# A two-layer hybrid decoder trunk: seven changes to the order of work around the norm, the first attention, the last retention and the end

## The chip, the core and the metric

The kernel runs on one core of a Trainium2 chip. A core has several engines that run side by side, each with its own queue of instructions: TensorE (PE) multiplies matrices into PSUM banks and loads its stationary operand separately (PEld), VectorE (DVE) and ScalarE (ACT) do elementwise work, GpSimd (POOL) does the same more slowly, and SyncE (SP) issues the transfers between memory and the core's on-chip buffers. The metric is the device time of one execution in microseconds (us); lower is better.

## What is computed

The reference, cut to what matters. There are 528 tokens (16 meta tokens and 512 of the sequence), a width of 1024, two layers, 8 attention heads of 64 and 4 retention heads of 128.

```python
def hybrid_layer(h, attn_norm_g, w_in, b_fgate, ret_gn_g, w_out,
                 ffn_norm_g, w_gate, w_up, w_down, cos, sin):
    xn = rmsnorm(h, attn_norm_g)
    proj = jnp.einsum('bld,dc->blc', xn, w_in)
    fq, fk, fv, flog, rq, rk, rv, rg = jnp.split(proj, SPLIT_POINTS, axis=-1)
    logf = jax.nn.log_sigmoid(flog.astype(jnp.float32) + b_fgate.astype(jnp.float32))
    fox_out = fox_attention(fq.reshape(fshape), fk.reshape(fshape), fv.reshape(fshape), logf)
    rq_ = rotate(rq.reshape(rshape), cos, sin)
    rk_ = rotate(rk.reshape(rshape), cos, sin) * (RET_HEAD_DIM ** -0.5)
    ret = retention_chunkwise(rq_, rk_, rv.reshape(rshape))
    ret = head_groupnorm(ret, ret_gn_g).astype(h.dtype)
    ret_out = jax.nn.silu(rg) * ret
    mix = jnp.concatenate([fox_out, ret_out], axis=-1)
    h = h + jnp.einsum('blc,cd->bld', mix, w_out)
    hn = rmsnorm(h, ffn_norm_g)
    ff = jax.nn.silu(jnp.einsum('bld,df->blf', hn, w_gate)) * jnp.einsum('bld,df->blf', hn, w_up)
    return h + jnp.einsum('blf,fd->bld', ff, w_down)
```

The attention adds the cumulative sum of `logf` to its scores: `logit[t,s] = q_t.k_s/sqrt(Dh) + c[t] - c[s]`. After the two layers a last rmsnorm is applied and the meta tokens are dropped.

## The kernel before

Activations lie with their features on the 128 partitions and the tokens along the row: `h` is 8 tiles of 128x528. For precision every operand of a matmul is split into a rounded high part and a rest (`split`, L142: a cast on ACT, a subtraction on DVE), and a product is three matmuls: high by high, rest by high, high by rest. Weights are split in the same way (`whi` by ACT, `wlo` by POOL or DVE; L192, L195) from a ring of three fetched blocks `raw` (L159).

A **dense step** (L218) is the product of one 128-row chunk of a weight block with one chunk of the activations: three matmuls for each of the two halves of the 528 tokens. Eight steps make a block of 128 outputs. Each layer runs four groups of columns, then the output projection, then the feed-forward part.

The order of PE is the order of the program text (`tc.manual_schedule`, L1350): the list `plan` in `layer` (L1247) holds all steps of a layer, and `run` (L233) issues them one by one. The order of the other engines is made by a scheduler, which follows the program but moves forward what stands under `tc.high_priority()`, and leaves alone what `pin` (L308) keeps in program order. So where PE's steps stand also sets where the work behind them stands on ACT and DVE.

The parts of a layer that matter here:

- **Start and norm.** `squares` (L327) sums the squares of `h`; `first_parts` (L1310) splits the sum into `sqh` and `sql`; `rstd` adds it over the partitions with two matmuls (L291) and makes the norm factor `R` by a logarithm (L296), an exponential (L297) and one Newton step on DVE (L298 to L301). Dense steps don't wait for `R`; it is applied to their results. `qk` is the list of the query and key steps of the first pair of attention heads, a query and a key step in turn, 16 in all; `v` holds the 8 value steps.
- **Gates.** `forget_gates` (L369, matmuls L381) multiplies out the 8 forget gates; two copies (L387) and two additions (L388) join the two halves of each result into `z`. `forget_sums` (L391) scales `z` by `R`, takes the log sigmoid, and scans it along the tokens (L401). The sums go to memory (`cdr`), and each head's row comes back as a broadcast over 128 partitions, `bc` (L501).
- **Attention** (`fox_steps`, L474), for a pair of heads: `values` transposes the values in five matmuls (L420) and splits them into `vv` (L487, L488); `scores` (L511) for a block of queries, with a mask (L517), a reduction with `bc` on DVE (L518) and an exponential on ACT (L531); block -1 is that of the meta tokens, with four small operations of its own (L547, L548, L557, L559); `turn` transposes and splits the weights into `pth` and `ptl`; `product` (L584) multiplies them with the values.
- **Retention** (`ret_steps`, L666): `values` (L420 again, then L680 and L681), `scores` (L717), `product` (L751, and L748 as its last matmul), a head norm with the same `col_rstd` (statistics L291, then L296, L297, L298 to L301, L787), `weigh` (L780, times the gate, whose `silu` is L409), and `gate`, which splits the result into a mix tile `mxh`, `mxl`. The mix tiles are what the output projection multiplies.
- **Places.** `merge` (L247) puts these steps among the dense steps: a step with the place 7 goes ahead of the eighth dense step of its stretch. `spread(main, a, b)` spreads a list evenly over the places from a to b. `ret_places` gives ten places: values, the first two scores, first product, third scores, two products, and last weigh, head norm and gate.
- **PSUM.** Results lie in two rings: `psd`, two pairs of banks for dense steps, and `psa`, four banks for everything else. A step that takes a bank waits until the last reader of the step four allocations earlier is done.
- **End.** The last norm is worked out in two parts of columns. For the second part (240 columns), `square_b` squares each tile (L1130), `sum_b` adds five of them up in `acc` (L1133), and three stay single. `sums` (L1159) adds over the partitions, `root` (L1147) and `newton` (L1151, L1153, L1155) make the factor, `out` multiplies (L1137) and sends (L1138). `after_0` to `after_7` stand behind the units of the last product, whose results are added to `h` by L1095.

ACT holds one table of functions at a time. Logarithm, exponential and `silu` are not all in one table; where the next function needs another, an `ACT_TABLE_LOAD` stands ahead of it.

Of the kernel before, what the change touches and what calls it, by code (L numbers as in the profile page):

```python
# [10 lines left out]
F32 = mybir.dt.float32  # L11
F32R = mybir.dt.float32r
AF = mybir.ActivationFunctionType
ALU = mybir.AluOpType
# [25 lines left out]
def hybrid_kernel(ctx, tc, x_t, w_in, w_fl, w_out, w_gate, w_up, w_down, vecs, b_fg, rope, decay, mask, ident, out_t):  # L40
    nc = tc.nc
# [15 lines left out]
    bfg = const.tile([FH, DEPTH], F32, name="bfg")  # L57
# [202 lines left out]
    def psum_a():  # L260
        return psa.tile([128, 512], F32, name="psa", tag="psa")
# [65 lines left out]
    def squares(st, cols, pinned=False, att=True):  # L327
        c = slice(cols[0][0], cols[-1][1])
        acc = tt("ss")
        for k in range(NK):  # L330
            if k == 0:
                first = nc.scalar.activation(acc[:, c], h[0][:, c], AF.Square)
                if pinned:
                    tc.keep_in_program_order(first)
            else:
                sq = tt("sq")
                more = nc.scalar.activation(sq[:, c], h[k][:, c], AF.Square)
                if pinned:
                    tc.keep_in_program_order(more)
                with ExitStack() if att else tc.high_priority():  # L340
                    nc.vector.tensor_add(acc[:, c], acc[:, c], sq[:, c])
        if pinned:
            st["acc"] = acc
            return
        with ExitStack() if att else tc.high_priority():
            st["parts"] = col_parts(acc, cols)
# [44 lines left out]
    def forget_sums(l, st):  # L391
        z = st["z"]
        z2 = tt("z2")[0:FH]
        with ExitStack() if l else tc.high_priority():
            nc.vector.scalar_tensor_tensor(z, z, RSC, st["R"][0:FH, :], ALU.mult, ALU.mult)
            nc.scalar.activation(z2, z, AF.Abs, bias=bfg[:, l:l + 1])
            nc.scalar.activation(z2, z2, AF.Exp, scale=-1.0)
            nc.scalar.activation(z2, z2, AF.Ln, bias=onec[0:FH])
        nc.vector.tensor_scalar(z, z, bfg[:, l:l + 1], 0.0, ALU.add, ALU.min)
        nc.vector.tensor_sub(z, z2, z)  # L400
        nc.vector.tensor_tensor_scan(z2, z, z, 0.0, ALU.add, ALU.max)  # L401
        st["cdr"] = tc.dram_tile([FH, T], F32, name=f"cdr{l}")
        nc.sync.dma_start(st["cdr"], z2)

# [410 lines left out]
    def ffn(l, st, real, last):  # L815
# [269 lines left out]
        else:  # L1085
# [4 lines left out]
            na, nb = PA[1] - PA[0], PB[1] - PB[0]  # L1090
            fin = {}
# [40 lines left out]
            def sum_b(m):  # L1132
                pin(nc.vector.tensor_add(fin["acc"], fin["acc"], fin["sq", m]))  # L1133
# [6 lines left out]
            def out_a(k):  # L1140
                out(fin["ya"][k // HB][:, k % HB:k % HB + 2], fin["ra"], k, *PA)
# [15 lines left out]
            def sums(v, parts):  # L1157
                for i, t in enumerate(parts):
                    nc.tensor.matmul(v, ones if t.dtype == F32R else ones.bitcast(F32), t, start=(i == 0), stop=(i == len(parts) - 1))  # L1159
# [39 lines left out]
            def after_4():  # L1199
                sum_b(3)  # L1200
                square_b(4)
                out_a(2)
                scale_b(1)

            def after_5():
                sum_b(4)
                square_b(5)
                hi, lo = tt("sqh", F32R)[:, 0:nb], tt("sql", F32R)[:, 0:nb]
                pin(nc.scalar.copy(hi, fin["acc"]))
                fin["b"] = hi, lo  # L1210
                scale_b(2)

            def after_6():
                hi, lo = fin["b"]
                pin(nc.vector.tensor_sub(lo, fin["acc"], hi.bitcast(F32)))
                square_b(6)

            def after_7():
                hi, lo = fin["b"]
                square_b(7)  # L1220
                v = psum_a()[:, 0:nb]
                sums(v, (fin["one"][0], hi, lo, fin["one"][1], fin["one"][2]))
                out_a(4)
                out_a(6)
                scale_b(3)
                root(fin["rb"], v)
                scale_b(4, 5, 6, 7)
# [19 lines left out]
    def layer(l):  # L1247
# [3 lines left out]
        ly, ff = {"wait": []}, {}  # L1251
# [19 lines left out]
        plan = []  # L1271
# [42 lines left out]
        sums = [lambda: forget_sums(l, ly)]  # L1314
        plan = [lambda: enter_att(l), start]
        if l == 0:
            plan += [lambda: squares(ly, FULL, True, False)] + qk[:6] + qk[6:] + [first_parts] + gates + stats + [lambda: ly["wait"].pop(0)()] + sums + [lambda: ly["wait"].pop(0)()]
        else:
            plan += [lambda: squares(ly, FULL)] + q[:7] + stats + q[7:] + gates + sums + k
        plan += v + [ropes]  # L1320

        def ret_places(hd, *places):

            f = rs[hd]
            return list(zip(places, (f[0], f[1], f[2], f[4], f[3], f[5], f[6], f[7], f[8], f[9])))

        for g in range(2):
            main, rest = fs[g]
            m0, r0, places = (((7, 31), (34, 40.5), (13, 33.5, 35.5, 37.5, 39, 40.5, 43, 44, 47.5, 48)),
                              ((0.5, 31.5), (32, 40), (13, 33.5, 35.5, 39.5, 39, 41.5, 43, 44, 47.5, 48)))[g]  # L1330
            plan += merge(rd(g, "vqkg") + sum(fd(g + 1), []),
                          spread(main, *m0), spread(rest, *r0), ret_places(g, *places))
# [7 lines left out]
        base += op[0:3] + op[4:7] + op[8:11] + op[12:15]  # L1340
        plan += merge(base, spread(main, 2, 46.5), spread(rest, 51, 56),
                      ret_places(2, 26, 23.5, 24.5, 32, 28, 33.5, 36, 56.5, 40.5, 57.5),
                      ret_places(3, 52, 45.5, 47.5, 57.5, 55.5, 58.5, 60, 64.1, 63, 64.2))
        plan += [op[3], op[7], op[11], op[15]] + op[16:]
        up = ffn(l, ff, real, real)
        plan += [lambda: enter("ffn"), start_ffn] + up
# [2 lines left out]
    plan = [f for l in range(DEPTH) for f in layer(l)]  # L1349
# [75 lines left out]
```

## Time and profile before

| | |
|---|---|
| time, median of 3 runs | 1272.59 us (1272.03 to 1273.82) |
| the profiled execution | span 1270.1 us |
| instructions | 23589 |
| PE busy | 1252.6 us |
| DVE busy | 1003.8 us |
| ACT busy | 694.5 us |
| POOL busy | 263.3 us |
| longest waits of PE | 1.7 us (product, L584), 1.6 us (first matmul of the program, L1278), 1.6 us (values, L420) |

The span of the profiled execution begins with its first instruction and ends with its last, and the times of the table's first row contain what lies around it. In the rows of the timeline that the prediction shows, the first number is the start in us from the start of the span, the second the duration of the group, then come the engine, the line of the program, the operation, the output and the inputs by their names in the program, the shapes, and the number of instructions in the group; in brackets stands how long the engine idled ahead of it and what ended that. Groups overlap slightly, since instructions are pipelined.

### The profile page before, as it was taken

The page shows a single profiled execution, that of the slowest core. Times are in us where ns is not written, and L with a number is a line of the kernel's source. Part 1 is how long each engine was busy: PE and PEld are TensorE (multiplying, and loading weights), DVE is VectorE, ACT ScalarE, POOL GpSimd, SP SyncE. Part 2 cuts the span into 40 slices and gives each one's busy share as a digit, 9 for nine tenths or more (in the row PEclk, how much of TensorE's full clock was granted, in tenths as well). Part 3 has the DMA queues.
Part 4 walks back from the last instruction along what each step waited for, and adds up shares of the span by engine and source line. Part 5 has one row for each costly group of instructions (what it writes and reads, how often), then busy time and mean ns, then how long its engine had stood idle before and what let it go on. Part 6 is the DMA issues. An engine that isn't in the chain of part 4 may idle for free.

```text
span 1270.1 us, 23589 instructions
## 1 busy us (share of the span) xinstructions
PE 1252.6 (99%) x9225; PEld 1193.1 (94%) x9225; DVE 1003.8 (79%) x1866; ACT 694.5 (55%) x1284; POOL 263.3 (21%) x524
## 2 busy tenths in 40 slices
PE   9999999999999999999999999999999999999997
PEld 8899999999999999999998989998789999999996
DVE  7877856879988888887786877568899888888867
ACT  7666556676444444444465665457764444444445
POOL 3355546420000000000025546454100000000000
PEclk9999999999999999999999999999999999999999
DMA  6322222213323232322323122221223333333321
GB/s 218 93 68 84 83 94 75 68 68 116 106 96 100 100 100 100 100 100 84 101 76 114 63 101 84 77 91 67 100 91 126 101 100 101 100 100 100 100 84 67
DMA packets 45679, 120.56 MB, mean 95 GB/s; under 512 B 5360, under 2 KB 12272, under 8 KB 45568
## 3 DMA queue, kind: packets, MB, share of 16 engines
q1 hardware_dynamic: 45136, 118.77, 28.3%
q8 instruction: 72, 1.18, 0.4%
q14 instruction: 39, 0.32, 0.1%
q10 hardware_dynamic: 432, 0.29, 0.1%
HBM read 116.91 MB, written 2.13 MB: 94 GB/s over the span
## 4 chain that ended last, share of the span: by engine, by line
PE 89%; DVE 5%; ACT 4%; DMA 1%; issue 1%; ACTq 0%; DVEq 0%; SPq 0%
PE psd L218 27%; PE psa L902 18%; PE psd L1037 14%; PE psd L902 13%; PE psa L218 5%; PE psa L1037 4%; PE psa L420 2%; PE psa L511 1%; PE psa L584 1%; PE psa L717 1%; PE psa L751 1%; DMA bc<-cdr 1%; PE psa L381 1%; ACT whi L192 1%; DVE pr L518 0%
## 5 line engine op out<-in xcount | busy, mean ns | idle before, releaser
L195 POOL TENSOR_TENSOR wlo<-raw,whi 128x128 fp32r<-128x128 f32 x504 | 259.1, 550 | 288.8 <-ACT whi L192 287.3
L218 PE MATMUL psd<-xh,whi 128*128 128x264 f32 (+1 forms) x792 | 195.6, 314 | 0.4 <-ACT whi L192 0.4
L218 PE MATMUL psd<-xl,whi 128*128 128x264 f32 (+1 forms) x792 | 186.3, 302 | 0.6 <-DVE xl L321 0.6
L218 PE MATMUL psd<-xh,wlo 128*128 128x264 f32 (+1 forms) x792 | 186.7, 303 | 0.0
L218 PEld LDWEIGHTS psd<-xh,whi 128*128 128x128 f32 x792 | 128.2, 189 | 5.2 <-ACT whi L192 0.8
L218 PEld LDWEIGHTS psd<-xh,wlo 128*128 128x128 f32 x792 | 127.0, 188 | 6.3 <-DVE wlo L195 0.6
L218 PEld LDWEIGHTS psd<-xl,whi 128*128 128x128 f32 x792 | 127.6, 189 | 5.2 <-DVE xl L321 1.2
L192 ACT CAST whi<-raw 128x512 fp32r<-128x512 f32 (+1 forms) x168 | 98.2, 613 | 45.7 <-PE psd L218 31.5
L890 ACT CAST whi<-raw 128x1024 fp32r<-128x1024 f32 (+2 forms) x62 | 54.8, 884 | 50.3 <-PE psd L902 37.0
L890 ACT CAST fwhi<-raw 128x1024 fp32r<-128x1024 f32 (+2 forms) x62 | 55.6, 897 | 47.9 <-PE psd L902 40.1
L891 DVE TENSOR_TENSOR fwlo<-raw,fwhi 128x1024 fp32r<-128x1024 f32 (+2 forms) x62 | 64.0, 1032 | 11.7 <-ACT fwhi L890 11.6
L85 POOL MEMSET kl<- 64x528 f32 x2 | 1.1, 534 | 345.5 <-PE psa L902 345.5
L891 DVE TENSOR_TENSOR wlo<-raw,whi 128x1024 fp32r<-128x1024 f32 (+2 forms) x62 | 62.9, 1014 | 12.2 <-ACT whi L890 12.1
L902 PE MATMUL psa<-th,whi 128*128 128x264 f32 (+1 forms) x232 | 65.4, 282 | 0.0
L902 PE MATMUL psa<-th,wlo 128*128 128x264 f32 (+1 forms) x232 | 65.4, 282 | 0.0
L902 PE MATMUL psa<-tl,whi 128*128 128x264 f32 (+1 forms) x232 | 65.3, 282 | 0.0
L902 PE MATMUL psa<-th,fwhi 128*128 128x264 f32 (+1 forms) x224 | 63.4, 283 | 0.0
L902 PE MATMUL psa<-tl,fwhi 128*128 128x264 f32 (+1 forms) x224 | 63.3, 283 | 0.0
L902 PE MATMUL psa<-th,fwlo 128*128 128x264 f32 (+1 forms) x224 | 63.2, 282 | 0.0
L531 ACT ACTIVATE pr<-pr,nmax 128x144 f32<-128x144 f32 (+1 forms) x64 | 36.9, 576 | 43.2 <-DVE nmax L518 31.2
L890 ACT CAST fwhi<-S 128x1024 fp32r<-128x1024 f32 x20 | 21.0, 1049 | 68.6 <-PE psa L902 66.5
L968 ACT COPY e<-psa 128x264 f32<-128x264 f32 (+1 forms) x114 | 42.9, 376 | 27.7 <-PE psa L902 23.6
(356 smaller groups left out, 4036.6 us busy)
## 6 DMA issues: line engine op xcount, KB each, us to landing
raw<-w_in SPq DMA_DIRECT2D x54, 512.0 KB, 3.5
raw<-w_gate SPq DMA_DIRECT2D x44, 512.0 KB, 4.0
fraw<-w_up SPq DMA_DIRECT2D x38, 512.0 KB, 3.4
raw<-w_down SPq DMA_DIRECT2D x64, 256.0 KB, 2.7
raw<-w_out SPq DMA_DIRECT2D x16, 512.0 KB, 3.4
raw<-w_down SPq DMA_DIRECT2D x32, 192.0 KB, 2.5
bc<-cdr SPq DMA_DIRECT2D x16, 264.0 KB, 3.4
raw<-w_up SPq DMA_DIRECT2D x6, 512.0 KB, 3.5
```

Source lines behind the costliest of these rows:

```text
L192: pin(nc.scalar.copy(hi, job["raw"][:, c0:c1]), pinned)
L195: pin(sub(lo[:, c:c + step], job["raw"][:, c0 + c:c0 + c + step], hi[:, c:c + step].bitcast(F32)), pinned)
L218: nc.tensor.matmul(ps[1][b][:, 0:c1 - c0], w[:, wk, :], x[:, c0:c1], start=(k == 0 and i == 0), stop=(k == n - 1 and i == 2))
L381: nc.tensor.matmul(ps[:, 0:c1 - c0], wf[k // HB][:, k % HB, :], st["x"][k][part][:, c0:c1], start=(i == 0), stop=(i == 2 * NK - 1))
L420: nc.tensor.transpose(ps[:, 128 * j:128 * j + 128], src[:, o:o + 128], idt)
L511: nc.tensor.matmul(sc[0:nq, 0:c1 - c0], st["q"][s][:, q0:q0 + nq], kk[:, c0:c1], start=(i == 0), stop=(i == 1))
L531: nc.scalar.activation(pr, pr, AF.Exp, bias=nmax[0:nq], scale=-1.0, accum_out=rsum)
L890: nc.scalar.copy(hi, src)
L891: nc.vector.tensor_sub(lo, src, hi.bitcast(F32))
L902: nc.tensor.matmul(bank()[:, 0:b.shape[-1]], a[:, o + k, :], b, start=(fresh and k == 0 and i == 0), stop=(k == n - 1 and i == 2), skip_gr ...
L968: nc.scalar.copy(self.t["e"][:, i], self.t["x"][:, 0:w])
L1037: nc.tensor.matmul(v[:, 0:c1 - c0], a[:, s * n + k, :], b[:, c0:c1], start=(k == 0 and i == 0), stop=(k == n - 1 and i == 2))
```

## The change

Seven places of the order, and the operand of one sum.

```diff
     def forget_sums(l, st):
-        with ExitStack() if l else tc.high_priority():
+        with tc.high_priority():
             nc.vector.scalar_tensor_tensor(z, z, RSC, st["R"][0:FH, :], ALU.mult, ALU.mult)
...
-        nc.vector.tensor_scalar(z, z, bfg[:, l:l + 1], 0.0, ALU.add, ALU.min)
-        nc.vector.tensor_sub(z, z2, z)
-        nc.vector.tensor_tensor_scan(z2, z, z, 0.0, ALU.add, ALU.max)
+            nc.vector.tensor_scalar(z, z, bfg[:, l:l + 1], 0.0, ALU.add, ALU.min)
+            nc.vector.tensor_sub(z, z2, z)
+            nc.vector.tensor_tensor_scan(z2, z, z, 0.0, ALU.add, ALU.max)
...
             def after_4():
                 sum_b(3)
                 square_b(4)
-                out_a(2)
                 scale_b(1)
             def after_5():
+                square_b(5)
+                scale_b(2)
+
+            def after_6():
                 sum_b(4)
-                square_b(5)
-                hi, lo = tt("sqh", F32R)[:, 0:nb], tt("sql", F32R)[:, 0:nb]
-                pin(nc.scalar.copy(hi, fin["acc"]))
-                fin["b"] = hi, lo
-                scale_b(2)
-
-            def after_6():
-                hi, lo = fin["b"]
-                pin(nc.vector.tensor_sub(lo, fin["acc"], hi.bitcast(F32)))
                 square_b(6)
             def after_7():
-                hi, lo = fin["b"]
                 square_b(7)
                 v = psum_a()[:, 0:nb]
-                sums(v, (fin["one"][0], hi, lo, fin["one"][1], fin["one"][2]))
+                sums(v, [fin["one"][0], fin["acc"]] + fin["one"][1:])
+                out_a(2)
                 out_a(4)
...
-            plan += [lambda: squares(ly, FULL, True, False)] + qk[:6] + qk[6:] + [first_parts] + gates + stats + [lambda: ly["wait"].pop(0)()] + sums + [lambda: ly["wait"].pop(0)()]
+            plan += [lambda: squares(ly, FULL, True, False)] + qk[:-2] + [first_parts] + gates + stats + qk[-2:] + sums + [lambda: ly["wait"].pop(0)()] * 2
...
-            m0, r0, places = (((7, 31), (34, 40.5), (13, 33.5, 35.5, 37.5, 39, 40.5, 43, 44, 47.5, 48)),
+            m0, r0, places = (((10, 32.5), (35, 41), (13, 33.5, 35.5, 38, 39, 41, 43.5, 44, 47.5, 48)),
...
-                      ret_places(3, 52, 45.5, 47.5, 57.5, 55.5, 58.5, 60, 64.1, 63, 64.2))
+                      ret_places(3, 52, 45.5, 47.5, 57.5, 55.5, 59, 61.5, 65.6, 64.5, 65.7))
```

In the line of `plan`, `wait` holds what is done with the results of the query and of the key steps, which in layer 0 is put off until `R` is there. The places of the first pair of heads and of the last retention head hold for both layers.

How the order of the engines moves, at three places. First ACT in the norm of layer 0; `z` is the gates' result, `sqh` the high part of the sum of squares, `R` the norm factor, `qs` the split queries. Before:

```order
L143 CAST sqh<-ss 128x528
L192 CAST whi<-raw 128x512 x2
L387 COPY z_396<-psa 8x264 x2
L296 ACTIVATE R<-psa,epsc 128x264 x2
L192 CAST whi<-raw 128x512
L297 ACTIVATE R<-R 128x528
L192 CAST whi<-raw 128x512
L439 CAST qs_418<-tq 64x528
```

Now:

```order
L387 COPY z_384<-psa 8x264 x2
L143 CAST sqh<-ss 128x528
L296 ACTIVATE R<-psa,epsc 128x264 x2
L192 CAST whi<-raw 128x512
L297 ACTIVATE R<-R 128x528
L192 CAST whi<-raw 128x512 x3
L396 ACTIVATE z_416<-z,bfg 8x528
L397 ACTIVATE z_416<-z_416 8x528
```

The copies of `z` stand ahead of the cast of `sqh`, and on DVE likewise their additions ahead of `sql`. On PE the last query and the last key step (`xh_197`) stand behind the statistics.

Second, DVE at the first scores of layer 0, from the first reduction with `bc`, that of the meta rows (`pm_116`), on; `ISA` is the reduction with its running minimum. Before:

```order
L518 ISA pm_116,nmax<-psa,bc 16x16
L518 ISA nmax 16x1
L518 ISA pr,nmax<-psa,bc 128x144
L518 ISA nmax 128x1
L488 TENSOR_TENSOR vv_613<-psa,vv_613 128x4x64
L547 RECIPROCAL rsum<-rsum 16x1
L517 TENSOR_TENSOR psa<-psa,msk 128x128
L548 TENSOR_SCALAR pm_116<-pm_116,rsum 16x16
L518 ISA pr,nmax<-psa,bc 128x272
L518 ISA nmax 128x1
L488 TENSOR_TENSOR vv_614<-psa,vv_614 128x4x64
```

Now, from the meta rows' third small operation on:

```order
L557 STREAM_TRANSPOSE pm<-pm_116 32x32
L559 TENSOR_TENSOR pth<-pm,pth 16x16
L517 TENSOR_TENSOR psa<-psa,msk 128x128
L518 ISA pr,nmax<-psa,bc 128x144
L518 ISA nmax 128x1
L488 TENSOR_TENSOR vv_636<-psa,vv_636 128x4x64
L680 TENSOR_REDUCE mean<-psa 128x4
L680 TENSOR_REDUCE mean<-psa 128x1
L681 SCALAR_TENSOR_TENSOR sq<-mean,psa 128x512
L681 SCALAR_TENSOR_TENSOR sq<-mean,psa 128x128
L488 TENSOR_TENSOR vv_637<-psa,vv_637 128x4x64
```

The meta rows' four operations stand ahead of the first full score's mask and reduction, and the second half of the attention values (`vv_614`, now `vv_637`) stands behind the means of the retention values. On PE the transposes of both kinds of values stand back to back:

```order
L420 MATMUL psa<-idt,pd_107 128x128 x5
L420 MATMUL psa<-idt,pd_108 128x128 x5
L218 MATMUL psd<-xh_189,whi 128x264 x2
L218 MATMUL psd<-xl_190,whi 128x264 x2
L218 MATMUL psd<-xh_189,wlo 128x264 x2
L511 MATMUL psa<-kh_438,qs_430 128x272
```

`pd_107` are the attention's values, `pd_108` those of the retention; before, 13 rows of dense steps and scores stood between the two.

Third, ACT at the last retention of layer 0; `r` is the factor of the head norm, `sg` the gate, `mxh` the last mix tile. Before:

```order
L764 ACTIVATE sqh<-d 128x528
L296 ACTIVATE r<-psa,epsc 128x264 x2
L192 CAST whi<-raw 128x512
L297 ACTIVATE r<-r 128x528
L409 ACT_TABLE_LOAD
L409 ACTIVATE sg<-sg 128x528
L411 ACT_TABLE_LOAD
L192 CAST whi<-raw 128x512
L143 CAST mxh_3899<-d 128x528
```

Now:

```order
L764 ACTIVATE sqh<-d 128x528
L192 CAST whi<-raw 128x512 x2
L296 ACTIVATE r<-psa,epsc 128x264 x2
L409 ACT_TABLE_LOAD
L409 ACTIVATE sg<-sg 128x528
L297 ACT_TABLE_LOAD
L297 ACTIVATE r<-r 128x528
L411 ACT_TABLE_LOAD
L143 CAST mxh_3914<-d 128x528
```

The exponential (L297) stands behind the gate's `silu` (L409) and has a table load of its own; layer 1 shows the same. On PE the last two products (L751 with 272 and 144 columns) stand two dense steps later, and the statistics (L291) likewise.

More of the change, by code (lines that the diff above doesn't have):

```diff
@@ L1201, in after_4 @@
                 square_b(4)
-                out_a(2)
                 scale_b(1)
             def after_5():
-                sum_b(4)
                 square_b(5)
-                hi, lo = tt("sqh", F32R)[:, 0:nb], tt("sql", F32R)[:, 0:nb]
-                pin(nc.scalar.copy(hi, fin["acc"]))
-                fin["b"] = hi, lo
                 scale_b(2)
             def after_6():
-                hi, lo = fin["b"]
-                pin(nc.vector.tensor_sub(lo, fin["acc"], hi.bitcast(F32)))
+                sum_b(4)
                 square_b(6)
             def after_7():
-                hi, lo = fin["b"]
                 square_b(7)
                 v = psum_a()[:, 0:nb]
-                sums(v, (fin["one"][0], hi, lo, fin["one"][1], fin["one"][2]))
+                sums(v, [fin["one"][0], fin["acc"]] + fin["one"][1:])
+                out_a(2)
                 out_a(4)
```

## The prediction

> **What bounds the kernel now.** I read the page's busy shares first, then its chain of work that ended last.
>
> ```profile
> PE 1252.6 (99%) x9225; PEld 1193.1 (94%) x9225; DVE 1003.8 (79%) x1866; ACT 694.5 (55%) x1284; POOL 263.3 (21%) x524
> PE 89%; DVE 5%; ACT 4%; DMA 1%; issue 1%; ACTq 0%; DVEq 0%; SPq 0%
> ```
>
> TensorE (PE) is busy 99% of a span of 1270.1 us, so only what PE waits for, what it runs at a lower clock, and the tail behind its last matmul can be won or lost. The change alters almost no matmul, it alters waits. So the next view is PE's list of waits (who waited for what: total us, times, longest):
>
> ```profile
> PE psa L584 <- DVE ptl L144: 1.7, 1, 1.7
> PE psa L420 <- DVE vv L488: 1.6, 1, 1.6
> PE psa L511 <- DVE kl L454: 0.6, 1, 0.6
> PE psa L751 <- DVE rsl L144: 0.6, 2, 0.4
> PE psa L511 <- DVE nmax L518: 0.6, 1, 0.6
> ```
>
> With the two waits shown under A and F these are what the edits can reach, about 6 us. The third view, the engines by stretches, shows a further cost, a clock drop behind the longest wait (columns: window, length; busy PE, PEld, DVE, ACT, POOL; granted clock, DMA share, GB/s):
>
> ```profile
> 58.00:60.00 2.00, 1.21 (x5) 1.15 (x6) 1.69 (x5) 1.18 (x5) 0.87 (x2) 0.83 0.15 20
> 60.00:62.00 2.00, 2.00 (x11) 2.00 (x10) 0.59 (x1) 0.58 (x1) 0.00 (x0) 0.50 0.63 242
> 62.00:64.00 2.00, 2.00 (x16) 2.00 (x15) 1.19 (x6) 0.11 (x1) 0.00 (x0) 0.82 0.00 0
> 678.00:680.00 2.00, 0.52 (x5) 0.28 (x3) 1.04 (x5) 1.20 (x6) 1.10 (x3) 1.00 0.04 14
> ```
>
> The clock is 0.50 at 60 to 62 us, right behind the 1.7 us wait; it stays 1.00 in the window of the 1.6 us wait (678 to 680). A drop costs 2 x 0.50 + 2 x 0.18 = 1.4 us. So a wait of about 1.6 us stands at the edge: once it dropped the clock, once not.
>
> The Trainium skill, "TensorE: Matmul & The Clock Gate", Part 1 on the clock gate, says that the clock falls to half after an idle window of about 3.4 us. By that none of the new waits below (2.4 us at most) would drop it, and each drop in the sum would be nothing. This trace disagrees: a wait of 1.7 us was followed by 0.50.
>
> **A: the first layer's norm (last query and key step behind the statistics).**
>
> ```profile
> 21.95 0.41 PE L291 MATMUL psa<-sqh,ones 128*128 128x264 f32 x2
> 22.99 0.73 PE L218 MATMUL psa<-xh,mxh 128*128 128x264 f32 x2 [0.39 <-DVE z L388]
> 20.41 0.64 ACT L143 CAST sqh<-ss 128x528 fp32r<-128x528 f32 x1 [1.82 <-DVE ss L341]
> 22.11 0.64 ACT L387 COPY z<-psa 8x264 f32<-8x264 f32 x2
> 22.51 0.76 DVE L388 TENSOR_TENSOR z<-psa,z 8x264 f32<-8x264 f32 x2 [0.72 <-ACT z L387]
> ```
>
> Two dense steps of 0.73 us (three rows of x2 each, a row every 0.24 us, as 273.11 and 273.35 under C) leave the place ahead of the gates, so the gates end at 21.95 - 1.46 = 20.49. But ACT now copies z ahead of the cast of sqh, and DVE adds z ahead of sql. The copies run from 20.56 to 21.20, sqh to 21.88, and PE waits 1.4 us for it. DVE adds z until 21.9; sql, an operation of 0.7 us, ends at 22.6, and the second statistics matmul waits 0.5 us more. Then come the two steps, and v, without its wait of 0.39 and the slow row behind it (0.73 for 0.41: a restart costs up to 0.3, and I take 0.2 where no row shows it). 1.9 of new idle less 0.9 (0.39, 0.33 and 0.17 of issue): **A = +1.0**. The norm factor R comes 0.2 us later, and the gates' sums, which go to memory and come back as a broadcast bc, keep their time, since their first step needs R.
>
> **B: the first attention of layer 0 (places 7 to 31 become 10 to 32.5).**
>
> ```profile
> 39.44 0.16 DVE L518 CUSTOM_DVE_ANT_0 pm<-psa,bc 16x16 f32<-16x16 f32 x1 [1.72 <-DMA bc<-cdr]
> 39.95 0.40 ACT L531 ACTIVATE pr<-pr,nmax 128x144 f32<-128x144 f32 x1
> 40.35 0.34 ACT L487 CAST vv<-psa 128x256 fp32r<-128x256 f32 x1
> 43.08 0.88 DVE L680 TENSOR_REDUCE mean<-psa 128x4 f32<-128x512 f32 x2
> 43.88 0.68 DVE L681 SCALAR_TENSOR_TENSOR sq<-mean,psa 128x512 f32<-128x512 f32 x1
> 51.83 7.40 SPq L159 DMA_DIRECT2D raw<-w_in  x2
> ```
>
> By step counts PE's first score falls at 37.5 now, the next at 39.0, the transposes of the attention values at 39.9. The waits for kl, for nmax and for ptl can go, with 0.2 of restart each and the drop: 0.6 + 0.6 + 1.7 + 0.6 + 1.4 = 4.9 us of gain. But bc still lands at 39.4, and the order has two new turns. First, the five transposes of the retention values stand right behind those of the attention values, so in the ring of four PSUM banks they need the banks of both first scores; and on DVE four small operations of the meta rows, which alternate with ACT, now come ahead of the reduction of the first full score. I walk that to 41.8, so PE's fifth transpose waits from 40.65 to 42.0: 1.35. Second, the next score, due at 42.95, needs the bank of the attention values, and its last reader on DVE now stands behind the retention means: exponential on ACT until 42.4, cast until 42.8, subtraction until 43.25, L680 until 44.1, L681 (two) until 44.95, the last subtraction until 45.3. PE waits 2.4 us; the score after that 0.6. Together 4.35, and 2.4 is well above the length that dropped the clock, so +1.4, of which the 0.6 comes back, since a slow PE needs that score later. **A + B = 1.0 + 4.35 + 1.4 - 0.6 - 4.9 = +1.25.** Bounds: no drop, +0.45; new waits half as long and no drop, -1.7; the wait for ptl kept besides, +3.2. On SP one weight fetch now stands ahead of the third broadcast; it is issued at 51.83, and that broadcast is first read by the next pair's scores at 62: nothing.
>
> **C and D: the last retention of each layer (places 58.5 to 64.2 become 59 to 65.7).** Layer 0:
>
> ```profile
> 263.73 0.85 ACT L296 ACTIVATE r<-psa,epsc 128x264 f32<-128x264 f32 x2 [1.39 <-PE psa L291]
> 264.47 0.62 ACT L192 CAST whi<-raw 128x512 fp32r<-128x512 f32 x1
> 264.98 0.65 ACT L297 ACTIVATE r<-r 128x528 f32<-128x528 f32 x1
> 265.65 1.28 ACT L409 ACT_TABLE_LOAD   x1
> 266.94 0.65 ACT L409 ACTIVATE sg<-sg 128x528 f32<-128x528 f32 x1
> 269.81 0.64 ACT L143 CAST mxh<-d 128x528 fp32r<-128x528 f32 x1 [0.28 <-DVE d L780]
> 265.67 0.95 DVE L298 TENSOR_TENSOR nwt<-r 128x528 f32<-128x528 f32 x1 [0.37 <-ACT r L297]
> 260.17 0.40 PE L751 MATMUL psa<-rsl,rvh 128*128 128x272 f32 x1 [0.23 <-DVE rsl L144]
> 273.11 0.40 PE L218 MATMUL psd<-mxh,whi 128*128 128x264 f32 x2
> 273.35 0.40 PE L218 MATMUL psd<-mxl,whi 128*128 128x264 f32 x2
> ```
>
> At 273.11 PE first reads the last mix tile, which is cast by 269.81 + 0.64 = 270.45: 2.6 us of slack. Two steps later, the last product no longer waits for rsl (0.3 with restart), and the statistics and Ln come 1.46 - 0.29 = 1.17 later, at 264.90. Behind Ln the order on ACT is now load, silu, load, Exp, load, cast, where it was Ln, Exp, load, silu, load: Exp stands behind the gate's silu and needs a table load of its own. Ln until 265.64 (0.74, the distance of the first two rows), load 266.92, silu 267.59, load 268.88, Exp 269.53, and DVE's nwt starts at 269.57. From nwt to mxh it was 269.81 - 265.67 = 4.14, so mxh runs from 273.71 to 274.35 and mxl until 275.1. PE wants mxh at 273.11 - 0.29 = 272.82, waits 1.53, then 0.5 for mxl: **C = 2.03 - 0.29 = +1.75**. The slack hides the 1.17, not also two loads and a silu (3.2) ahead of Exp. The whole rest of ACT and DVE stands behind that chain, but PE is the one that waits. Layer 1:
>
> ```profile
> 890.39 0.69 ACT L296 ACTIVATE r<-psa,epsc 128x512 f32<-128x512 f32 x1 [1.45 <-PE psa L291]
> 892.15 0.94 DVE L298 TENSOR_TENSOR nwt<-r 128x512 f32<-128x512 f32 x1 [0.37 <-ACT r L297]
> 896.16 0.62 ACT L143 CAST mxh<-d 128x512 fp32r<-128x512 f32 x1 [0.16 <-DVE d L780]
> 899.25 0.39 PE L218 MATMUL psd<-mxh,whi 128*128 128x512 f32 x1
> ```
>
> Steps of 0.70 here, and a wait of 0.4 with 0.16 of restart gone: Ln at 890.39 + 1.40 - 0.56 = 891.23, until 891.82, two loads, silu and Exp to 895.7, mxh 4.01 behind nwt, 899.7 to 900.34, mxl until 901.05. PE wants it at 898.69 and waits 1.65, then 0.45: **D = 2.1 - 0.56 = +1.55**. Bounds for each of C and D: 0 if all of it hides, +3.2 with a drop behind it. Waits of 1.53 and 1.65 lie at the edge, so I take half a drop for each.
>
> The Trainium skill, "ScalarE: Activation LUTs", What ACT_TABLE_LOAD costs, gives 1283 ns a load and 1380 ns of drain. The load agrees (1.28); a drain does not show, as silu starts at 266.94, 0.01 us behind the end of its load. With a drain at the one further switch of each layer the sum would be 2.8 us higher.
>
> **E: the first attention of layer 1.** The wait of 1.57 for vv goes, with up to 0.3 of restart, as the scores move three steps and the retention values ahead. A score then waits for a bank that those values held; I put it at 0.7, by the two waits of 0.6 for scores above. **E = -1.2** (bounds 0 and -1.9). The gates' sums get priority here too, but the order of the engines stays: nothing.
>
> **F: the end.**
>
> ```profile
> 1258.76 0.72 DVE L1137 TENSOR_TENSOR th<-th,e 128x544 f32<-128x544 f32 x1
> 1260.56 0.41 DVE L1215 TENSOR_TENSOR sql<-S,sqh 128x240 fp32r<-128x240 f32 x1
> 1260.28 0.67 PE L1159 MATMUL psa<-S,ones 128*128 128x240 f32 x2 [0.74 <-ACT S L1130]
> ```
>
> The 0.72 scaling moves behind the last residual addition and is covered by the squares, the matmuls and the root. sql and the cast to sqh go; the sum goes in unsplit, in as many matmuls (8). So the operand PE waited for is there when its last unit ends, at 1260.28 - 0.74 = 1259.54: 0.74 and a restart go, **F = -0.9** (bounds -1.1, the two DVE operations, and 0).
>
> **Sum:** 1.25 + 1.75 + 1.55 - 1.2 - 0.9 = +2.45 with no drop at C and D; a half drop each adds 1.4, of which I give back half, because a slow PE stops waiting for mxl and for what follows. +3.1 on the span gives 1273.2. The median of the runs, 1272.59, lies 2.5 above the profiled span, which changes nothing in the difference. I forecast +3.0: **1275.6 us**.
>
> **Rivals.**
> *Nothing that can be told*: no drop anywhere, and A + B between its lower bounds, -0.6: -0.6 + 3.3 - 2.1 = +0.6, 1273.2. For it: 678 us, where such a wait left the clock at 1.00.
> *Faster*: the retention means and the meta rows' operations find gaps on DVE that my walk lacks, and B's new waits vanish: 1.0 - 4.9 + 3.3 - 2.1 = -2.7, 1269.9. It decides once the fifth transpose finds its bank free at 40.65. Against it: the first reduction can't start before bc, at 39.4.
> *Both out-projection waits drop the clock*: 2.45 + 2.8 = +5.2, 1277.8; with ptl's wait kept as well +7.2, 1279.8. For it: 1.7 us sufficed at 58 us.
> *The table order costs nothing*, as the loads run ahead during ACT's wait for Ln: C and D at -0.3 and -0.6, sum -1.75, 1270.8. Against it: before, each load starts only behind the operation ahead of it (264.98 + 0.65, then 265.65).
>
> **How the numbers follow.** Chances: forecast 0.42, both drop 0.17, nothing 0.23, table order 0.08, faster 0.10. A measurement of this kernel can tell about 0.2% (2.5 us), so faster is below 1270.1 and slower above 1275.1. The forecast's own range is 1274.2 to 1277; about three quarters of it is slower (0.32). With both drops and a rest of the third case slower is 0.52, faster 0.11 and same 0.37. The range, 1270.4 to 1279.4, leaves out most of the fast case and the end of the slow one.
>
> **What would show it.** In the changed trace: a wait of PE for sqh of about 1.4 us near 21 us (A); waits at a transpose near 41 and at a score near 44 us, the one for ptl gone (B); PE waiting for mxh near 273 and 899 us with three table loads around silu and Exp, and the clock behind (C, D); no wait at the end's sums (F). I am wrong if PE reads the last mix without a wait, or if no score waits near 43 us.

## The result, and the profile after

| | before | after |
|---|---|---|
| median time | 1272.56 us (five runs) | 1278.19 us |
| ratio to before | | 1.0043, 95% interval 1.0029 to 1.0056 |
| span of the profiled execution | 1270.1 us | 1275.3 us |

One of the five executions of the changed kernel took 4351.5 us; it counts in the median and not in the ratio, and the other four have a median of 1277.8 us. The change makes the kernel slower by some 5.5 us (5.6 between the medians, 1.0043 in the ratio), and the spans of the two profiled executions differ by 5.2. PE's list of waits in the changed kernel:

```profile
PE psa L420 <- DVE nmax L518: 3.8, 2, 2.1
PE psd L218 <- ACT mxh L143: 2.0, 2, 1.4
PE psa L511 <- DVE sq L681: 1.3, 1, 1.3
PE psa L291 <- ACT sqh L143: 1.1, 1, 1.1
PE psd L218 <- DVE mxl L144: 0.5, 2, 0.2
PE psa L291 <- DVE sql L144: 0.4, 1, 0.4
PE psa L1159 <- ACT S L1130: 0.2, 1, 0.2
```

All five waits of the list before are gone, and the one at the end fell from 0.74 to 0.21. In their place stand two waits at transposes and one at a score in the first attention of layer 0 (5.1 together; they end at 44.07, 46.39 and 49.03 us), the waits for the last mix tile (2.5), and those at the statistics (1.5). The clock shows where more went (the engines by stretches, columns as before; the granted clock stands ahead of the last two numbers):

```profile
22.00:24.00 2.00, 1.71 (x10) 1.71 (x11) 0.23 (x1) 1.28 (x4) 0.00 (x0) 0.75 0.73 250
24.00:26.00 2.00, 2.00 (x11) 2.00 (x11) 1.30 (x3) 2.00 (x5) 1.83 (x4) 0.50 0.00 0
26.00:28.00 2.00, 2.00 (x17) 2.00 (x16) 1.93 (x4) 0.18 (x1) 2.00 (x4) 0.90 0.00 0
46.00:48.00 2.00, 1.38 (x7) 1.10 (x7) 1.17 (x4) 1.25 (x5) 0.00 (x0) 0.72 0.04 14
48.00:50.00 2.00, 0.97 (x4) 1.00 (x5) 1.56 (x6) 1.07 (x3) 0.00 (x0) 0.50 0.00 0
50.00:52.00 2.00, 2.00 (x10) 1.99 (x9) 0.94 (x6) 0.87 (x4) 0.00 (x0) 0.50 0.00 0
52.00:54.00 2.00, 2.00 (x12) 2.00 (x11) 1.52 (x5) 1.20 (x2) 0.53 (x2) 0.57 0.00 0
278.00:280.00 2.00, 1.14 (x7) 0.71 (x6) 1.12 (x3) 0.63 (x1) 0.00 (x0) 1.00 0.00 0
904.00:906.00 2.00, 1.12 (x4) 0.72 (x5) 0.69 (x1) 0.60 (x1) 0.00 (x0) 1.00 0.00 0
```

In this execution the clock drops behind the norm and in the first attention, and not behind the waits for the last mix tile. Where a window of 2 us has the clock c, it loses 2 x (1 - c): the first drop costs 0.50 + 1.00 + 0.20 = 1.7 us, the second 0.56 + 1.00 + 1.00 + 0.86 = 3.4. To place the 5.2 us, I took the start of the same matmul in both timelines at several points:

| point | before | after | later by |
|---|---|---|---|
| first pair of layer 0 done (L593) | 76.59 | 81.97 | 5.38 |
| fourth pair of layer 0 done (L593) | 254.66 | 259.73 | 5.07 |
| layer 0, first feed-forward products by `th` (L902) | 326.14 | 332.70 | 6.56 |
| first pair of layer 1 done (L593) | 709.83 | 714.68 | 4.85 |
| fourth pair of layer 1 done (L593) | 881.38 | 886.18 | 4.80 |
| layer 1, the same feed-forward products | 950.54 | 956.55 | 6.01 |
| last matmul of the last product (L902) | 1259.27 | 1265.28 | 6.01 |
| end of the span | 1270.1 | 1275.3 | 5.2 |

Read as differences of the last column: norm and first attention of layer 0 +5.1, its last retention +1.5, first attention of layer 1 -1.7, its last retention +1.2, end -0.8. So the first 80 us hold nearly the whole loss, and there SP's queue has changed. SP before:

```profile
21.01 10.74 SPq L159 DMA_DIRECT2D raw<-w_in  x3
34.44 0.30 SPq L403 DMA_DIRECT2D cdr<-z  x1
35.93 0.81 SPq L501 DMA_DIRECT2D bc<-cdr  x2
```

SP after:

```profile
20.98 16.03 SPq L159 DMA_DIRECT2D raw<-w_in  x3
37.10 0.30 SPq L403 DMA_DIRECT2D cdr<-z  x1
40.59 0.81 SPq L501 DMA_DIRECT2D bc<-cdr  x2
```

A group's second number is the time from the start of its first issue to the end of its last. The issue of the third weight fetch ends at 31.75 before, and at 37.01 after; the gates' sums `cdr` stand behind it in the queue, and though their scan ends at 33.01 + 1.40 = 34.41, they leave at 37.10. The transfer is slower too: the broadcast, which waits for it, follows 3.5 us behind instead of 1.5; 512 KB of weights were issued just ahead of it, and they land at 40.36, just before the broadcast leaves at 40.59. DVE after, at the scan and at the first reduction that reads the broadcast:

```profile
33.01 1.40 DVE L401 TENSOR_TENSOR_SCAN z<-z 8x528 f32<-8x528 f32 x1
43.84 0.16 DVE L518 CUSTOM_DVE_ANT_0 pm<-psa,bc 16x16 f32<-16x16 f32 x1 [4.71 <-DMA bc<-cdr]
```

43.84 instead of 39.44. And why is the fetch late? Its buffer comes free when POOL has split the block that lies in it. POOL before, then POOL after:

```profile
21.65 9.74 POOL L195 TENSOR_TENSOR wlo<-raw,whi 128x128 fp32r<-128x128 f32 x16 [19.68 <-ACT whi L192]
```

```profile
24.17 12.48 POOL L195 TENSOR_TENSOR wlo<-raw,whi 128x128 fp32r<-128x128 f32 x16 [22.20 <-ACT whi L192]
```

POOL begins 2.5 us later, since the weights that it splits are cast later, and its 16 subtractions take 2.7 us longer. POOL does not idle between them; single ones last longer (0.46 us at the least, the longest 1.59 before and 2.07 after), and why is not shown, though it goes with the moved step (12.5 us in only_qk and fetch_other_queue, 9.7 in after_old_qk and only_fox0, which have the old place). So the late start explains about half of the delay of the fetch. PE after, at the last reads of the high parts by the moved query step and the moved key step, and ACT's casts of the next weights into the same two buffers:

```profile
22.88 0.55 PE L218 MATMUL psd<-xl,whi 128*128 128x264 f32 x2
24.11 0.64 PE L218 MATMUL psd<-xl,whi 128*128 128x264 f32 x2
```

```profile
23.47 0.62 ACT L192 CAST whi<-raw 128x512 fp32r<-128x512 f32 x1
24.54 1.64 ACT L192 CAST whi<-raw 128x512 fp32r<-128x512 f32 x3
```

The first cast starts at 23.47, as the first read ends (22.88 + 0.55 = 23.43). The last two, into the other buffer, start at 25.05, behind the end of the second read (24.11 + 0.64 = 24.75). Before, the casts of these weights began at 20.95; PE had turned to the gates at 18.08, and the buffers were free. So the moved steps kept the buffers. The casts also have a later place on ACT, behind the logarithm (L296) instead of ahead of it, and no run separates the two: in fetch_other_queue, below, the first buffer is free at 23.03 and its cast starts at 23.20, right behind the logarithm.

### The profile page after: what moved, and what is told of

Same layout as the page of the kernel before. It is cut to its first block, busy times and chain, and to the rows that moved or that the text cites. A ratio compares the mean times of both kernels' runs of the same rounds, so it can differ in the third digit from the quotient of the medians.

```text
span 1275.3 us, 23593 instructions
## 1 busy us (share of the span) xinstructions
PE 1255.4 (98%) x9225; PEld 1195.9 (94%) x9225; DVE 1000.3 (78%) x1865; ACT 697.7 (55%) x1285; POOL 267.3 (21%) x524
## 4 chain that ended last, share of the span: by engine, by line
PE 93%; DVE 3%; ACT 2%; DMA 2%; issue 0%; SPq 0%; DVEq 0%; ACTq 0%
PE psd L218 30%; PE psa L902 18%; PE psd L1037 14%; PE psd L902 13%; PE psa L218 4%; PE psa L1037 4%; PE psa L420 2%; PE psa L511 2%; PE psa L584 2%; PE psa L717 1%; PE psa L751 1%; DMA raw<-w_in 1%; PE psa L291 0%; DMA dec<-decay 0%; PE psa L593 0%
## 5 line engine op out<-in xcount | busy, mean ns | idle before, releaser
L195 POOL TENSOR_TENSOR wlo<-raw,whi 128x128 fp32r<-128x128 f32 x504 | 263.1, 558 | 279.1 <-ACT whi L192 278.1
L891 DVE TENSOR_TENSOR fwlo<-raw,fwhi 128x1024 fp32r<-128x1024 f32 (+2 forms) x62 | 64.0, 1032 | 11.0 <-ACT fwhi L890 10.6
L902 PE MATMUL psa<-th,whi 128*128 128x264 f32 (+1 forms) x232 | 65.4, 282 | 0.0
L902 PE MATMUL psa<-th,wlo 128*128 128x264 f32 (+1 forms) x232 | 65.4, 282 | 0.0
L902 PE MATMUL psa<-tl,whi 128*128 128x264 f32 (+1 forms) x232 | 65.3, 282 | 0.0
L902 PE MATMUL psa<-th,fwhi 128*128 128x264 f32 (+1 forms) x224 | 63.4, 283 | 0.0
L902 PE MATMUL psa<-tl,fwhi 128*128 128x264 f32 (+1 forms) x224 | 63.3, 283 | 0.0
L902 PE MATMUL psa<-th,fwlo 128*128 128x264 f32 (+1 forms) x224 | 63.2, 282 | 0.0
```

The source lines that it names most:

```text
L195: pin(sub(lo[:, c:c + step], job["raw"][:, c0 + c:c0 + c + step], hi[:, c:c + step].bitcast(F32)), pinned)
L891: nc.vector.tensor_sub(lo, src, hi.bitcast(F32))
L902: nc.tensor.matmul(bank()[:, 0:b.shape[-1]], a[:, o + k, :], b, start=(fresh and k == 0 and i == 0), stop=(k == n - 1 and i == 2), skip_gr ...
```

## The experiments

Each ratio is to the kernel before as it ran beside the experiment (1272.11 us beside the first four, 1272.65 beside the last four). Two theories of the first 80 us were set against each other. **Queue theory**: the moved query and key step hold the weight buffers, so the splitting, the fetch, the sums behind it on SP and the broadcast are late. **Bank theory**, the one of the prediction: the waits come from the back-to-back transposes and from DVE's order, wherever the broadcast lands.

**after_old_qk**: the change without its moved step.

```diff
-            plan += [lambda: squares(ly, FULL, True, False)] + qk[:-2] + [first_parts] + gates + stats + qk[-2:] + sums + [lambda: ly["wait"].pop(0)()] * 2
+            plan += [lambda: squares(ly, FULL, True, False)] + qk[:6] + qk[6:] + [first_parts] + gates + stats + [lambda: ly["wait"].pop(0)()] + sums + [lambda: ly["wait"].pop(0)()]
```

> The change with the last query and key step back ahead of the gates; all else as changed. Queue theory (the moved steps hold both weight buffers until 25 us, so the next weights are split late, their block of raw comes free late, the third fetch on SP issues at 36.7 instead of 31.7, and the gates' sums behind it go out at 37.1 instead of 34.4): sums out at 34.4 to 34.6, bc read at 39.4 to 39.7, no wait for sqh, clock 1.00 at 24 us; time 4 us or more below the changed kernel, some 1273 to 1274. Bank theory (the waits at 44 to 49 us come from the transposes standing back to back and DVE's order, wherever bc lands): only the norm's own loss goes, some 1.5 us, time 1276.5 to 1277.

Measured: 1271.48 us, ratio to before 0.9996 (0.9988 to 1.0005), span 1269.5: by the ratios 6.0 us below the changed kernel, by the spans 5.8. Its SP queue and DVE:

```profile
34.54 0.30 SPq L403 DMA_DIRECT2D cdr<-z  x1
```

```profile
39.31 0.16 DVE L518 CUSTOM_DVE_ANT_0 pm<-psa,bc 16x16 f32<-16x16 f32 x1 [1.69 <-DMA bc<-cdr]
```

The sums leave on time and the broadcast is read at 39.31; the queue theory's numbers. Its time, 1273 to 1274, was too high by some 2 us; the bank theory had 1276.5 to 1277, and that is out. But its waits are there, in a smaller part; PE:

```profile
40.90 0.30 PE L420 MATMUL psa<-idt,pd 128*128 128x128 f32 x1 [0.69 <-DVE nmax L518]
43.91 0.36 PE L511 MATMUL psa<-kh,qs 128*128 128x272 f32 x1 [1.98 <-DVE sq L681]
```

0.7 and 2.0, where the prediction had 1.35, 2.4 and 0.6. The first pair of layer 0 is done 1.9 us earlier than before. In layer 1 the clock drops in this execution (0.50 at 900 to 902 us), behind the wait of 1.36 us for the last mix tile that left it at 1.00 in the changed kernel.

**only_qk**: the kernel before with only that move (the diff of the line above, the other way round).

> The kernel before with only the last query and key step moved behind the statistics. Queue theory: sums out near 37, bc read near 43.8, time 4 to 6 us above before (scores stand even earlier here than in the changed kernel). Bank theory: only the norm's wait, 1 to 1.5 us above before.

Measured: 1277.82 us, 1.0051 (1.0038 to 1.0063), span 1278.0. PE's waits:

```profile
PE psa L511 <- DVE nmax L518: 5.4, 1, 5.4
PE psa L291 <- ACT sqh L143: 1.1, 1, 1.1
```

```profile
44.55 0.16 DVE L518 CUSTOM_DVE_ANT_0 pm<-psa,bc 16x16 f32<-16x16 f32 x1 [5.99 <-DMA bc<-cdr]
```

The sums leave at 37.44, and the broadcast is read at 44.55: the queue theory's numbers again. One of the seven edits alone costs as much as the whole change: the score waits 5.4 us, the clock is 0.50 from 44 to 50 us, and the first pair is done 7.6 us late. (The profile is of an execution of 1279.81 us, 2.0 above the median, and has a second drop, 0.50 at 68 to 70 us.) The norm's own wait, which was all that the prediction charged to the move, is the smaller line.

**only_fox0**: the kernel before with only the places of the first pair changed, in layer 0 alone.

```diff
-            m0, r0, places = (((7, 31), (34, 40.5), (13, 33.5, 35.5, 37.5, 39, 40.5, 43, 44, 47.5, 48)),
+            m0, r0, places = (((10, 32.5), (35, 41), (13, 33.5, 35.5, 38, 39, 41, 43.5, 44, 47.5, 48)) if l == 0 else ((7, 31), (34, 40.5), (13, 33.5, 35.5, 37.5, 39, 40.5, 43, 44, 47.5, 48)),
```

> The kernel before with only the places of the first pair's attention and retention in layer 0 changed. Queue theory: bc read at 39.4 as before; the waits for kl, nmax and ptl and the clock drop at 60 to 62 us go (4.9), waits for banks near 42 to 45 come (2 to 4.3, with or without a drop of 1.4): between -2.5 and +0.5 against before. Bank theory: the full 3 to 4 us of the new waits with a drop, +0.5 to +2.

Measured: 1271.56 us, 0.9997 (0.9989 to 1.0006), span 1269.7: the queue theory's range, -2.5 to +0.5 against before, and not the bank theory's +0.5 to +2. The same two waits as above (0.60 and 1.98), and the clock behind them:

```profile
44.00:46.00 2.00, 1.99 (x10) 2.00 (x11) 1.38 (x7) 1.83 (x6) 0.00 (x0) 0.62 0.00 0
46.00:48.00 2.00, 2.00 (x11) 2.00 (x10) 1.53 (x5) 0.62 (x1) 0.00 (x0) 0.53 0.00 0
```

The first pair is done 0.3 us earlier than before; in after_old_qk, with the same waits and the clock at 1.00 in both windows, it was 1.9. The difference of 1.6 is the drop: 2 x 0.38 + 2 x 0.47 = 1.7.

**fetch_other_queue**: the changed kernel, with one weight fetch issued from POOL, behind the subtraction that frees its buffer, instead of from SP.

```diff
-                nc.sync.dma_start(job["raw"], job["src"]) if n == NK else \
+                (nc.gpsimd if j == 7 else nc.sync).dma_start(job["raw"], job["src"]) if n == NK else \
```

> The changed kernel, with the one weight fetch that stands ahead of the gates' sums on SP issued from POOL instead, behind the subtraction that frees its buffer. Queue theory: sums go out at 34.4 to 34.6 as soon as the scan ends, bc is read some 2.5 to 4 us earlier than 43.84, and the time falls by 1.5 to 4 us. If the sums are late for another reason (scan, priority), they go out at 37 as before and nothing falls.

Measured: 1273.24 us, 1.0014 (1.0005 to 1.0023), span 1270.6: by the ratios 3.7 us below the changed kernel, by the spans 4.7, around the upper end of what was expected (4). SP, POOL and DVE of this run:

```profile
34.19 0.30 SPq L403 DMA_DIRECT2D cdr<-z  x1
35.67 0.81 SPq L501 DMA_DIRECT2D bc<-cdr  x2
```

```profile
36.70 0.69 POOL L159 DMA_DIRECT2D raw<-w_in  x1 [0.30 <-POOL wlo L195]
```

```profile
39.02 0.16 DVE L518 CUSTOM_DVE_ANT_0 pm<-psa,bc 16x16 f32<-16x16 f32 x1 [1.25 <-DMA bc<-cdr]
```

The fetch is as late as in the changed kernel (36.70), and only the sums no longer stand behind it: the broadcast is read 4.8 us earlier. That shows the queue as the cause of the late sums. The first pair is done at 75.75 instead of 81.97, 6.2 us earlier. The clock is 1.00 at 20 to 28 and at 38 to 64 us in this run. So 1.7 of the 6.2 is the drop behind the norm, which is not the queue's: the waits ahead of it are nearly the same here (1.14 and 0.23). Some 4.5 is what the late sums cost, with the 3.4 of the drop behind their waits in it. A drop in layer 1 (0.51 at 900 to 902 us, behind the wait of 1.35 us for the last mix tile) takes 1.6 back. The norm's own loss is left: from the first matmul of the gates to the first dense step behind the values PE takes 16.12 to 29.66 here, 13.54 us with the two moved steps (1.46) in it, and 18.08 to 29.20 before, 11.12. That is +0.96, where the prediction had 1.0; in the changed kernel, with the drop, it is 16.25 to 31.46, +2.63.

**only_ret3**: the kernel before with only the places of the last retention head.

```diff
-                      ret_places(3, 52, 45.5, 47.5, 57.5, 55.5, 58.5, 60, 64.1, 63, 64.2))
+                      ret_places(3, 52, 45.5, 47.5, 57.5, 55.5, 59, 61.5, 65.6, 64.5, 65.7))
```

> The kernel before with only the places of the last retention head changed, both layers. Table theory (Exp behind silu and a third table load per layer make PE wait for the last mix tile): a load ahead of Exp, PE waits for mxh of 0.6 and 1.4 us as in the changed kernel, first feed-forward matmul +1.5 and second layer's +2.7 against before; time 2 to 3 us above before. If the places themselves gained and the loss came only on top of the late first layer, the time is not above before.

Measured: 1276.07 us, 1.0028 (1.0019 to 1.0038), span 1274.3. That is 3.4 us more than before, where 2 to 3 were expected. PE waits 2.0 for mxh, as in the changed kernel, and ACT has the same order. In layer 0 of the changed kernel it is:

```profile
270.62 1.28 ACT L409 ACT_TABLE_LOAD   x1
271.91 0.65 ACT L409 ACTIVATE sg<-sg 128x528 f32<-128x528 f32 x1
272.57 1.28 ACT L297 ACT_TABLE_LOAD   x1
273.87 0.64 ACT L297 ACTIVATE r<-r 128x528 f32<-128x528 f32 x1
274.53 1.28 ACT L411 ACT_TABLE_LOAD   x1
```

The feed-forward products start 1.0 us late in layer 0, on a profile that was 0.45 early ahead of it, so +1.5; in layer 1 the loss is 2.7 (from +1.53 to +4.25), where the changed kernel had 1.2. The wait of 1.36 for mxh is the same in both; this time the clock fell behind it:

```profile
902.00:904.00 2.00, 1.90 (x6) 1.59 (x7) 0.79 (x3) 0.44 (x1) 0.00 (x0) 0.73 0.03 8
904.00:906.00 2.00, 2.00 (x6) 1.51 (x6) 2.00 (x4) 1.32 (x3) 0.00 (x0) 0.50 0.00 0
```

**ret3_exp_first**: the same places, with the silu issued behind the head norm, and ACT's order of the two fixed.

```diff
             if hd > 1:
-                silu(sv(sg, real), LOGS)
+                st["silu"] = lambda: silu(sv(sg, real), LOGS, hd == 3)
+                if hd == 2:
+                    st.pop("silu")()
                 return
...
-            nc.scalar.activation(r[:, c_all], r[:, c_all], AF.Exp, scale=-0.5)
+            pin(nc.scalar.activation(r[:, c_all], r[:, c_all], AF.Exp, scale=-0.5), pinned)
...
             nc.vector.scalar_tensor_tensor(sv(d, real), sv(d, real), gn, sv(r, real), ALU.mult, ALU.mult)
+            if "silu" in st:
+                st.pop("silu")()
```

> The same places for the last retention head, but the gate's silu is issued behind the head norm's exponential, so that ACT's order is Ln, Exp, load, silu, load again. Table theory: no PE wait for mxh, two table loads, the wait for rsl gone: 0.3 and 0.56 us below before, time -0.5 to -1 against before. If the later places and not the order of the tables cost the time, it is as slow as the run without this repair, 2 to 3 us above before.

Measured: 1270.62 us, 0.9986 (0.9977 to 0.9996), 2.0 us below before between the medians, where 0.5 to 1 was expected; the spans differ by 0.7. ACT in layer 0 (the gating product, L780 before, is L782 here):

```profile
265.02 0.85 ACT L296 ACTIVATE r<-psa,epsc 128x264 f32<-128x264 f32 x2 [0.15 <-PE psa L291]
265.90 0.65 ACT L297 ACTIVATE r<-r 128x528 f32<-128x528 f32 x1
266.57 1.28 ACT L409 ACT_TABLE_LOAD   x1
267.86 0.65 ACT L409 ACTIVATE sg<-sg 128x528 f32<-128x528 f32 x1
268.52 1.28 ACT L411 ACT_TABLE_LOAD   x1
270.75 0.64 ACT L143 CAST mxh<-d 128x528 fp32r<-128x528 f32 x1 [0.94 <-DVE d L782]
```

The places are those of the change, the exponential stands ahead of silu, and mxh is cast at 270.75, more than 1.5 us before PE reads it at 272.99. No wait for mxh or rsl is left. The places were worth 0.5 us in layer 0 (from +0.35 to -0.12) and 0.8 in layer 1 (from +0.20 to -0.63); the table order had made them cost 1.5 and 1.2.

**end_and_l1**: the kernel before with the end of the change, the places of the first pair in layer 1 alone (the diff of only_fox0 with `l == 1`), and the priority of the sums.

> The kernel before with the end of the change, the places of the first pair in layer 1 alone, and the priority of the gates' sums. From the changed kernel's trace: layer 1's first attention -1.8, the end -0.8: 2.6 us below before, 1269.5 to 1270. If those gains existed only because earlier parts ran late, less than 1 us.

Measured: 1269.03 us, 0.9972 (0.9962 to 0.9982), 3.6 us below before, where 2.6 was expected. Layer 1's first attention gains 1.7 (from -1.67 to -3.39), the end 0.8 (span -4.3, last matmul -3.47). The remaining 1.7 comes from the first 80 us, where no place was changed, and most of it from the clock: the wait of PE for ptl is there as before, and the drop isn't. PE, and the window behind:

```profile
58.70 0.50 PE L584 MATMUL psa<-ptl,vv 128*128 128x512 f32 x1 [1.68 <-DVE ptl L144]
```

```profile
60.00:62.00 2.00, 2.00 (x19) 2.00 (x18) 1.26 (x5) 0.58 (x1) 0.00 (x0) 1.00 0.68 244
```

**all_but_qk**: the whole change without the moved step, with silu behind the exponential (the diffs of after_old_qk and ret3_exp_first).

> The whole change without the moved query and key step, and with silu behind Exp at the last retention. Sum of the parts: first attention -1.9 (or -0.3 with a clock drop), layer 1's first attention -1.8, end -0.8, last retentions -0.85: 3.7 to 5.3 us below before, 1267 to 1268.5. If the parts get in each other's way, no better than the run with only the end and layer 1's places.

Measured: 1267.27 us, 0.9960 (0.9945 to 0.9976), span 1265.1, with a clock drop at 44 to 46 us. It is 5.4 us faster than the kernel before, close to the 5.3 at the end of what was expected, and 10.6 to 10.9 faster than the changed one, and the best of all that ran.

## Why the prediction was right, and where its steps were not

The forecast was slower by 3.0 us, 1275.6 in a range of 1270.4 to 1279.4; the measured time is 1278.19, slower by 5.6. The direction and the range hold, but the largest part of the loss is one that the prediction had at nothing. By its terms:

- **A, the norm's own waits: +1.0.** Right: +0.96 in fetch_other_queue. The waits were 1.15 and 0.35 in the changed kernel (1.14 and 0.23 in fetch_other_queue) in place of 1.4 and 0.5. A clock drop of 1.7 us followed in the changed kernel (0.50 at 24 to 26 us), which the prediction had not put there.
- **"The gates' sums ... keep their time, since their first step needs R" is the step that failed.** The scan did keep its time (34.41). What was missed is that the moved dense steps also hold the weight buffers, and that the sums stand on SP behind a fetch which waits for one. Only the instructions moved were counted, not the buffers that they keep; on SP the prediction looked at the third broadcast alone. That was worth 4.4 us at the first reduction (43.84 instead of 39.44) and, with the clock drop behind its waits, some 4.5 us at the end of the first pair. only_qk shows that the moved step is the cause, fetch_other_queue that the queue passes it on.
- **B, the first attention: +0.25 with a drop, -0.55 without.** Measured with the sums on time, -0.3 with a drop (only_fox0) and -1.9 without (after_old_qk). The mechanism, a ring of four banks and DVE's order, is right; the waits were mis-sized at 4.35 instead of 2.7 in after_old_qk, and 3.3 in fetch_other_queue, which keeps the moved step. In after_old_qk the fifth transpose waited 0.7, as the reduction of the first full score began at 40.46, 1.15 us behind that of the meta rows; in fetch_other_queue it began at 41.85, where the prediction's walk had 41.8, and the waits were 1.74 and 1.60. The 0.6 at the last score occurred in neither.
- **C and D: +1.75 and +1.55, with half a drop each.** Measured +1.5 and +1.2, and no drop in the profiled execution of the changed kernel; the layer 1 wait of the same length did drop the clock in only_ret3, after_old_qk and fetch_other_queue. In layer 0 the wait for the last mix tile is 0.63 where the prediction had 1.53; two shorter waits (0.19 for `nwt`, 0.23 for `mxl`) and the slow rows behind all three make up the rest. The three loads and the exponential behind silu are there as forecast, and ret3_exp_first shows that the table order alone makes the loss. The rival that the order costs nothing is out.
- **E: -1.2.** Measured -1.7. The bank wait that I put at 0.7 does not show.
- **F: -0.9.** Measured -0.8.

So with the sums on time A and B together give -0.8 (75.75 against 76.59, in fetch_other_queue), and C to F 1.5 + 1.2 - 1.7 - 0.8 = +0.2: -0.6 in all, or +1.1 with one drop of the clock. That is the rival "nothing that can be told". The late sums with the drop behind them, 4.5, and the drop behind the norm, 1.7, make the 5.2 out of that (5.6 by this sum). That the forecast came out slower, and near the time, is therefore luck in good part: its own terms came to +3.1, and to -0.6 to +1.1 when measured without the late sums, which it had at nothing. A drop was priced at 1.4 us, which leaves out the 0.83 at 58 to 60 us; with it the drop before costs 0.34 + 1.00 + 0.36 = 1.7.

The rival "both out-projection waits drop the clock", 1277.8, is closest to the measured time, but its mechanism is not the one at work in the profiled execution: the clock was 1.00 at both places.

**What stays open:** what decides whether a wait drops the clock; the runs show only that its length alone does not. Open too is why POOL's subtractions took 2.7 us longer, which is half of the delay of the fetch.

## What to carry to other kernels

When a step on a busy engine is moved later, count what it holds as well as what it does. Here its weight buffers stayed occupied, the next weights were cast and split late, the fetch into their block waited at the head of its transfer queue, and the sums behind it left at 37.10 though they were ready at 34.41. Before a chain of small elementwise steps on ACT is moved, look at which table each function needs: two dense steps later was a gain of 0.5 and 0.8 us here, and turned into a loss of 1.5 and 1.2 because the exponential slipped behind a silu. The edits of a bundle should run alone or in small groups: here one cost as much as the whole, another lost, and the rest gave a faster kernel.

## What the runs showed of the hardware

A PE wait of the same length at the same matmul drops the clock in one run and not in the next: 1.69 us at the ptl product gave 0.50 before, 1.68 in end_and_l1 gave 1.00; 1.98 at the score gave 0.53 in only_fox0 and 1.00 in after_old_qk; 1.36 at the last mix tile gave 0.50 in only_ret3 and after_old_qk, 0.51 in fetch_other_queue (1.35 there) and 1.00 in the changed kernel. Up to the last product, each stretch of lower clock in these profiles adds up to the same loss, 1.7 us, or to twice that: 0.54 + 1.00 + 0.16 = 1.7 at 902 to 908 us in only_ret3, 0.98 + 0.72 = 1.7 at 900 to 904 in fetch_other_queue, 3.4 at 44 to 52 in only_qk and at 46 to 54 in the changed kernel. A loss of 1.7 at a clock of 0.50 is a stretch of 3.4 us. PE's own progress agrees: the drop behind the norm cost 2.63 - 0.96 = 1.67. So one drop alone moves one execution by 0.1%. The Trainium skill, "TensorE: Matmul & The Clock Gate", Part 1 on the clock gate, says that the window in which idleness is measured runs freely and isn't tied to the kernel; drops that come and go behind equal waits agree with that, though no run here shows the window itself.
